# A hybrid attention and DeltaNet layer: the order of the matmuls of attention and scan written out by hand

## The chip, the cores and the metric

The kernel runs on one core of a Trainium2 chip, in one launch. The metric is the device time in microseconds, the median of the runs; the profile is one further execution, with the hardware profiler on. Engines: TensorE (PE, with its weight loads PEld), VectorE (DVE), ScalarE (ACT), GpSimd (POOL), and SyncE (SP), which here only issues DMAs.

## The reference

One layer over 1024 latent tokens (16 rows of 64) and 256 context tokens, width 1024, in float32. After an adaptive RMS norm one projection feeds two branches.

```python
# neighbourhood attention, 8 heads of 64: every latent query sees an 8 x 16 window and all context keys
s_loc = einsum('bchd,bicjhd->bhcij', q_r, k_win) + bias      # bias: learned, by row and column offset
s_ctx = einsum('bchd,bnhd->bhcn', q_r, k_ctx)
p = softmax(concatenate([s_loc, s_ctx]))                     # one softmax over both
o_na = p_loc @ v_win + p_ctx @ v_ctx
# gated DeltaNet, 4 heads of 128, forward and backward, context first, then latent
v_new = u_n - w_n @ state
o_n   = q_n @ state + qk_n @ v_new
state = state * gl_n + k_n.T @ v_new
# both branches are gated and go through one output projection
y = concatenate([o_na * silu(na_z), rmsnorm(o_g) * silu(g_z)]) @ w_out
x = x + gate * rmsnorm(y, g_post)
```

## The kernel before

The program has three stages in time. The first makes norms, projections, convolutions and the inverses of the DeltaNet chunks, and leaves queries, keys, values, gates and the scan's operands in DRAM. The second runs attention and scan side by side. The third is the output product, `phase4`.

Most products are split: a number is held as a high and a low part (`hi`, `lo`, type `F32R`), and a product is two or three matmuls. A plain float32 matmul stands in the trace as two records.

**Attention** (`na_attn`, `na_unit`). The 8 heads make 4 pairs `p`. A pair has 2 row tiles `rt` of 4 column tiles `ct`, a unit of 128 queries each. In a unit the two heads `hh` are its half units. A half unit does this:

- POOL adds the bias `gt` and the mask `mk` to `gm` (L676, 288 columns for `ct` 0 and 3, 384 for 1 and 2).
- PE makes the context scores `pc` (L684) and the local ones `pl` (L688, whose keys `kv` are read from row order `(n r c)` as `(n c r)`, that is with a stride of 64 elements).
- DVE takes the maximum (L692) and adds `gm` (L693); ACT takes both exponentials (L694, L695).
- PE transposes the result back into `pl` and `pc` (L697, L702); DVE copies it to `tl` (L699), ACT to `tcx` (L704).

After both halves the value products add up in `po` (L710, L715). After four units the row tile is scaled: DVE multiplies `po` by the gate (L610), the reciprocal sums are spread by POOL (L618) and transposed by PE (`prt`, L621, in a buffer of tag `sl`), and DVE multiplies again (L623). `pc` and `pl` have two PSUM buffers each (tags `sc`, `sl`), `po` has one.

**Scan** (`delta_scan`). Four heads, each 10 steps, both directions `d` in a step. A direction's step is a chain: `pa = kq @ state` (L1133), `y` on DVE (L1134), `pa = tm @ y` (L1138), `vn` on ACT (L1140 or L1142), `pa = kd @ vn` (L1144), new state on DVE (L1147). From the third step on it also makes outputs in `pos` (L1152, L1153), which ACT and DVE add to `o` (L1156, L1159, L1160). A head's operands are loaded at its start (`tm`, `v`, `kt`, `kq` in two buffers, `qe` in one); at its end `o` is normalised, transposed (L1182) and gated.

**What sets the order.** `phase_b` steps two Python generators: after unit `u` the scan is advanced to `min(43, u * 1.40)` steps. That is the order in which the program is written. The order in each engine's queue is then made by a planner, which follows a timeline of its own with estimated costs: of what is ready it takes what was written first. So the products of attention and scan mix freely on PE, but the mix is fixed when the program is built. An ordering edge (`order(r, before)`) ties an instruction behind another on the same queue without a semaphore.

**W_out** is cast and split into `hi` and `lo` by halves of 512 columns (`split_w`: DMA to `wor`, ACT cast L647, POOL subtraction L648), in buffers that the attention's and the scan's tiles leave (`w_out_early`), the rest in `phase4`. `phase4` multiplies in the order `W_ORDER = [3, 0, 1, 2, 4, 5, 6, 7]`: block 3 is the last pair of attention, kept on chip (`split_m`, L659, L660); blocks 0, 1, 2, 4, 5, 6 come back from DRAM through two buffers; block 7 is the last head of the scan. The last steps of the scan may run inside `phase4`, up to its sixth block.

Of the kernel before, what the change touches and what calls it, by code (L numbers as in the profile page):

```python
# [11 lines left out]
F32 = mybir.dt.float32  # L12
# [127 lines left out]
class K:  # L140
    def __init__(self, tc, I, out, dbg=None):
        self.tc, self.nc, self.I, self.out = tc, tc.nc, I, out
        self.dbg = dbg or {}
        self.na_first = None
        self.gate = self.after = None
# [438 lines left out]

    def na_attn(self, na, ps):
        nc = self.nc
# [9 lines left out]
        nxt = load(0)  # L596
        for p in range(4):
            qk, gts, vv, zs = nxt
            for rt in range(2):
                sums = self.nw.tile([P, 4, 2, 2], F32, name=f"sums{p}_{rt}", tag="sums", bufs=2)  # L600
                po = ps.tile([P, 4, P], F32, name=f"po{p}_{rt}", tag="po", bufs=1)
                for ct in range(4):
                    self.na_unit(ps, p, rt, ct, qk, vv, gts, self.mk, sums, po)
                    if p < 3 and (rt, ct) == (0, 1):
                        self.gate = self.scan_loads if p == 0 else None
                        nxt = load(p + 1)
                        self.gate = None
                    yield
                zv = zs[:, 512 * rt:512 * rt + 512].rearrange("p (a t c) -> p a t c", a=8, t=4)
                nc.vector.tensor_tensor(zv, po.rearrange("p t (a c) -> p a t c", a=8), zv, ALU.mult)  # L610
                rs = self.nw.tile([P, 8], F32, name=f"rs{p}_{rt}", tag="rs", bufs=2)
                nc.vector.tensor_tensor(rs.rearrange("p (a b) -> p a b", a=4), sums[:, :, :, 0], sums[:, :, :, 1],
                                        ALU.add)
                nc.vector.tensor_scalar(rs, rs, 2.0, None, ALU.mult)
                nc.vector.reciprocal(rs, rs)

                rb = self.nw.tile([P, 640], F32, name=f"rb{p}_{rt}", tag="pt", bufs=3)[:, :512].rearrange("p (a b) -> p a b", a=8)
                nc.gpsimd.tensor_copy(rb, bc(rs.unsqueeze(2), [P, 8, 64]))  # L618
                pt = ps.tile([P, 512], F32, name=f"prt{p}_{rt}", tag="sl", bufs=2)
                for ct in range(4):  # L620
                    nc.tensor.transpose(pt[:, ct * P:(ct + 1) * P],  # L621
                                        rb[:, 2 * ct:2 * ct + 2, :].rearrange("p a b -> p (a b)"), self.ident)
                nc.vector.tensor_tensor(zv, pt.rearrange("p (t a c) -> p a t c", t=4, a=8), zv, ALU.mult)  # L623
            if p < 3:
                self.load(self.m_dram[P * p:P * p + P, :], zs)
            else:
                self.split_m(3, zs)
            if p == 2:
                self.w_out_early(self.pf, [("qh0", 8), ("ql0", 8), ("qh1", 8), ("ql1", 8), ("kk0", 10), ("kk1", 10)])

# [10 lines left out]
    def split_w(self, k, hi, lo):  # L641
        nc = self.nc
        hr, lr = hi.bitcast(F32R), lo.bitcast(F32R)
        for o in range(0, D, 512):
            raw = self.g3.tile([P, 512], F32, name=f"wor{k}_{o}", tag="wor", bufs=2)
            self.load(raw, self.I["w_out"][k * P:(k + 1) * P, o:o + 512], self.na_last)
            nc.scalar.copy(hr[:, o:o + 512], raw)  # L647
            nc.gpsimd.tensor_tensor(lr[:, o:o + 512], raw, hi[:, o:o + 512], ALU.subtract)  # L648
        self.wo[k] = (hr, lr)
# [13 lines left out]
    def na_unit(self, ps, p, rt, ct, qk, vv, gts, mk, sums, po):  # L663
# [6 lines left out]
        tls, tcs = [], []  # L670
        for hh in range(2):
            gt = gts[hh]
            gv = bass.AP(gt.tensor, gt[:, (4 * (1 - rt)) * 31 + GCOL0[ct]:].offset,
                         [list(gt.ap[0]), [4 * 31, 3], [1, nco], [31, 4]])
            gm = self.nw.tile([P, 384], F32, name=f"gm{p}_{u}_{hh}", tag="gm", bufs=2)
            nc.gpsimd.tensor_tensor(gm[:, :n].rearrange("p (n c r) -> p n c r", c=nco, r=4), gv,  # L676
                                    mk[:, mo:mo + n].rearrange("p (n c r) -> p n c r", c=nco, r=4), ALU.add)
            pcb = ps.tile([P, 512], F32, name=f"pc{p}_{u}_{hh}", tag="sc", bufs=2)
            pl = ps.tile([P, 512], F32, name=f"pl{p}_{u}_{hh}", tag="sl", bufs=2)
            pc = pcb[:, :256]  # L680
            pl3 = pl[:, :n].rearrange("p (n c r) -> p n c r", c=nco, r=4)
            qs, kk = qk[hh]
            for i, a in enumerate(qs):
                nc.tensor.matmul(pc, a[:, u * P:(u + 1) * P], kk[:, S:S + CT], start=(i == 0), stop=(i == 1))  # L684
            kv = kk[:, 256 * rt:256 * rt + 768].rearrange("p (n r c) -> p n c r", c=64, r=4)[
                :, :, KCOL0[ct]:KCOL0[ct] + nco, :]
            for i, a in enumerate(qs):
                nc.tensor.matmul(pl3, a[:, u * P:(u + 1) * P], kv, start=(i == 0), stop=(i == 1))  # L688
            mi = self.nw.tile([P, 1], F32, name=f"mi{p}_{u}_{hh}", tag="mi", bufs=4)
            nm = self.nw.tile([P, 1], F32, name=f"nm{p}_{u}_{hh}", tag="nm", bufs=4)  # L690
            pt = self.nw.tile([P, 640], F32, name=f"pt{p}_{u}_{hh}", tag="pt", bufs=3)
            nc.vector.tensor_reduce(mi, pc, AX.X, ALU.max, negate=True)  # L692
            nc.vector.tensor_tensor_reduce(pt[:, :n], pl[:, :n], gm[:, :n], -1.0, mi, ALU.add, ALU.min, nm)  # L693
            nc.scalar.activation(pt[:, :n], pt[:, :n], AF.Exp, bias=nm, scale=-1.0, accum_out=sums[:, ct, hh, 0:1])  # L694
            nc.scalar.activation(pt[:, 384:640], pc, AF.Exp, bias=nm, accum_out=sums[:, ct, hh, 1:2])  # L695
            for rc in range(3):
                nc.tensor.transpose(pl[:m, rc * P:(rc + 1) * P], pt[:, rc * m:(rc + 1) * m], self.ident)  # L697
            tl = self.nw.tile([P, 384], F32, name=f"tl{p}_{u}_{hh}", tag="tl", bufs=4)
            nc.vector.tensor_copy(tl[:m, :], pl[:m, :384])  # L699
            tls.append(tl)  # L700
            for cc in range(2):
                nc.tensor.transpose(pc[:, cc * P:(cc + 1) * P], pt[:, 384 + cc * P:384 + (cc + 1) * P], self.ident)  # L702
            tcx = self.nw.tile([P, 2, P], F32, name=f"tcx{p}_{u}_{hh}", tag="tcx", bufs=4)
            nc.scalar.copy(tcx.rearrange("p c q -> p (c q)"), pc)  # L704
            tcs.append(tcx)

        for cc in range(2):
            for hh in (1, 0):
                hb = 64 * hh
                nc.tensor.matmul(po[hb:hb + 64, ct, :], self.vcx[:, cc, P * p + hb:P * p + hb + 64], tcs[hh][:, cc, :],  # L710
                                 start=(cc == 0), stop=False, tile_position=(0, hb))
        for rc in range(3):
            for hh in (1, 0):
                hb = 64 * hh
                nc.tensor.matmul(po[hb:hb + 64, ct, :], vv[:m, ct, rt + rc, hb:hb + 64], tls[hh][:m, rc * P:(rc + 1) * P],  # L715
                                 start=False, stop=(rc == 2), tile_position=(0, hb))
# [375 lines left out]
    def delta_scan(self, g3, ps, h):  # L1092
# [9 lines left out]
        if h == 0:  # L1102
# [4 lines left out]
            nc.gpsimd.tensor_tensor(self.rho2, self.rho, self.rho, ALU.mult)  # L1107
            yield
        tm, qe = (w.rearrange("p (d t) c -> p d t c", d=2) for w in (tm, qe))
        o = g3.tile([P, 8, P], F32, name=f"o{h}", tag="o", bufs=2)  # L1110
        if h == 3:
            self.w_out_early(g3, [("o", 8), ("tm", 20)])
        order = [list(range(10)), [1, 0] + list(range(9, 1, -1))]
        seen = set()
        st = [None, None]
        chain = [ps.tile([P, 512], F32, name=f"pa{h}_{d}", tag=f"pa{d}", bufs=1)[:, :P] for d in range(2)]
        po = ps.tile([P, 2, 2, P], F32, name=f"pos{h}", tag="os", bufs=1)
# [276 lines left out]
```

## Time and profile before

| what | value |
| --- | --- |
| median of 3 runs | 895.79 us (891.43 to 896.62) |
| profiled execution, own time | 903.52 us |
| its span in the trace | 901.8 us, mean granted clock 0.971 |
| first stage, to the first scores | 0 to 559 us |
| attention and scan, to the first output product | 559 to 801 us |
| output product and closing tiles | 801 to 902 us |

A row of the timeline is: start, duration, engine, line, operation, output<-inputs, shapes, count, and in brackets the idle time before it with what ended that. A row of the waits is: who waited, for whom, microseconds in total, times, longest. A row of a stage is: its ends, its length, busy time and instructions of PE, PEld, DVE, ACT and POOL, then the granted clock, the DMA share and GB/s.

### The profile page before, as it was taken

To read this page: it belongs to the slowest core of one execution; us is meant where nothing else is said; L and a number is where in the kernel's file an instruction comes from. 1 tells how busy PE (TensorE), PEld (TensorE's weight loads), DVE (VectorE), ACT (ScalarE), POOL (GpSimd) and SP (SyncE) were. 2 spreads that over 40 slices of the span, in tenths; PEclk is the share of its full clock that TensorE was granted. 3 is DMA by queue.
4 is the path that set the end of the run, shared out by engine and by line. 5 is a ranking of instruction groups with operands and counts; after the bars stand their busy time and mean duration, and the time that the engine had idled before them with its cause. 6 is when DMAs were issued, how large, how long until landed. Compare 5 with 4: busy or idle time off the path is not lost.

```text
span 901.8 us, 16600 instructions
## 1 busy us (share of the span) xinstructions
PE 840.9 (93%) x6082; PEld 705.1 (78%) x6082; DVE 538.4 (60%) x1179; ACT 416.5 (46%) x1165; POOL 368.9 (41%) x431
## 2 busy tenths in 40 slices
PE   5999999999999989898989977999899997899996
PEld 3688887887888868688877867888788886788785
DVE  3453464556546699679639523677677776562442
ACT  4263536645644454552243533546456555642220
POOL 1332321724544532344512112757557568532210
PEclk9999999999999989998999986999999999999999
DMA  9686432265364544633899857989759233223251
GB/s 339 252 283 243 140 117 84 82 216 177 98 228 155 136 135 153 187 105 95 283 260 260 212 172 284 356 203 256 229 138 292 98 113 121 72 87 124 92 199 61
DMA packets 95176, 160.98 MB, mean 179 GB/s; under 512 B 28581, under 2 KB 55542, under 8 KB 92918
## 3 DMA queue, kind: packets, MB, share of 16 engines
q1 hardware_dynamic: 87606, 146.25, 52.0%
q10 hardware_dynamic: 7488, 13.67, 4.9%
q8 instruction: 48, 0.79, 0.4%
q14 instruction: 34, 0.28, 0.1%
HBM read 110.82 MB, written 52.42 MB: 181 GB/s over the span
## 4 chain that ended last, share of the span: by engine, by line
PE 62%; DVE 14%; DMA 11%; ACT 5%; issue 3%; SPq 3%; POOL 1%; DVEq 0%; ACTq 0%; POOLq 0%
PE py L1218 3%; PE py L1220 3%; PE py L1219 3%; DVE tb L1003 3%; DVE vb L1006 2%; PE pl L688 2%; PE po L715 2%; PE pl L697 2%; PE pz L464 2%; PE pz L460 2%; PE pz L465 2%; PE po L710 2%; PE pc L684 2%; DMA pm_dram<-pm 2%; DMA tm_dram<-tm 2%
## 5 line engine op out<-in xcount | busy, mean ns | idle before, releaser
L676 POOL TENSOR_TENSOR gm<-gt,mk 128x288 f32<-128x288 f32 (+1 forms) x64 | 64.3, 1008 | 35.4 <-DVE nm L693 35.1
L1125 POOL TENSOR_SCALAR kd<-kt,kd 128x128 f32<-128x128 f32 x72 | 43.2, 603 | 31.2 <-PE pa L1144 30.9
L694 ACT ACTIVATE pt<-pt,nm 128x288 f32<-128x288 f32 (+1 forms) x64 | 36.7, 574 | 30.0 <-DVE nm L693 29.4
L692 DVE TENSOR_REDUCE mi<-pc 128x1 f32<-128x256 f32 x64 | 26.7, 420 | 30.8 <-PE pc L684 30.3
L945 ACT ACTIVATE em<-em,gc 128x128 f32<-128x128 f32 x80 | 25.6, 391 | 34.6 <-DMA em<-gc_dram 24.5
L699 DVE COPY tl<-pl 96x384 f32<-96x384 f32 (+1 forms) x64 | 35.3, 551 | 10.0 <-PE pl L697 9.8
L464 PE MATMUL pz<-hl,wh_gz 128*128 128x512 f32 x96 | 40.2, 418 | 0.0
L697 PE MATMUL pl<-c,pt 128*96 128x128 f32 (+1 forms) x192 | 33.0, 281 | 7.6 <-ACT pt L694 7.6
L465 PE MATMUL pz<-hh,wl_gz 128*128 128x512 f32 x96 | 39.7, 414 | 0.0
L460 PE MATMUL pz<-hh,wh_gz 128*128 128x512 f32 x96 | 39.7, 413 | 0.0
L693 DVE CUSTOM_DVE_ANT_0 pt<-pl,gm,mi 128x288 f32<-128x288 f32 (+1 forms) x64 | 35.9, 562 | 4.2 <-PE pl L688 1.5
L1003 DVE TENSOR_TENSOR tb<-ab,vb 120x31 f32<-120x31 f32 (+15 forms) x62 | 32.2, 519 | 10.3 <-DMA ab<-ab_dram 8.8
L473 PE MATMUL pv<-wh_nv,hh 128*128 128x264 f32 x128 | 35.5, 296 | 2.8 <-ACT hh L262 1.9
L475 PE MATMUL pv<-wl_nv,hh 128*128 128x264 f32 x128 | 35.8, 289 | 1.4 <-DVE wl_nv L446 1.4
L474 PE MATMUL pv<-wh_nv,hl 128*128 128x264 f32 x128 | 36.8, 292 | 0.0
L812 DVE SCALAR_TENSOR_TENSOR acc_v<-xp_v,cols,acc_v 128x1282 f32<-128x1282 f32 x16 | 29.1, 1818 | 10.8 <-ACT acc_v L810 10.6
L964 POOL TENSOR_SCALAR_AFFINE_SELECT qe<-qe 128x256 f32<-128x256 f32 x32 | 25.5, 799 | 23.4 <-DVE qe L963 22.9
L704 ACT COPY tcx<-pc 128x256 f32<-128x256 f32 x64 | 23.5, 368 | 21.6 <-PE pc L702 21.1
L960 DVE SCALAR_TENSOR_TENSOR pm<-pk,beta,em 128x128 f32<-128x128 f32 x80 | 23.6, 343 | 15.8 <-PE pk L953 11.5
L1128 POOL TENSOR_SCALAR vb<-v,beta 128x128 f32<-128x128 f32 x40 | 24.1, 604 | 17.8 <-DVE y L1134 13.9
L697 PEld LDWEIGHTS pl<-c,pt 128*96 128x96 f32 (+1 forms) x192 | 22.1, 136 | 11.9 <-ACT pt L694 10.8
L1133 PE MATMUL pa<-s,kq 128*128 128x128 f32 x144 | 28.3, 285 | 2.0 <-DVE s L1147 1.4
(438 smaller groups left out, 2903.6 us busy)
## 6 DMA issues: line engine op xcount, KB each, us to landing
wada<-in_w_ada SPq DMA_DIRECT2D x16, 512.0 KB, 6.5
em<-gc_dram SPq DMA_DIRECT2D x20, 256.0 KB, 4.1
pm_dram<-pm SPq DMA_DIRECT2D x20, 256.0 KB, 2.8
pmf<-pm_dram SPq DMA_DIRECT2D x8, 640.0 KB, 5.9
tm_dram<-tm SPq DMA_DIRECT2D x8, 640.0 KB, 7.4
kk<-qk_dram SPq DMA_DIRECT2D x16, 320.0 KB, 10.8
tm<-tm_dram SPq DMA_DIRECT2D x4, 1280.0 KB
kq_dram<-kq SPq DMA_DIRECT2D x4, 1152.0 KB
```

What stands on the lines that cost most here:

```text
L460: r = nc.tensor.matmul(ps, wh, xh, start=(k == 0), stop=False)
L464: nc.tensor.matmul(ps, wh, xl, start=False, stop=False)
L465: nc.tensor.matmul(ps, wl, xh, start=False, stop=(k == KC - 1))
L473: nc.tensor.matmul(ps, xh, wh, start=(k == 0), stop=False)
L474: nc.tensor.matmul(ps, xl, wh, start=False, stop=False)
L475: nc.tensor.matmul(ps, xh, wl, start=False, stop=(k == KC - 1))
L676: nc.gpsimd.tensor_tensor(gm[:, :n].rearrange("p (n c r) -> p n c r", c=nco, r=4), gv, mk[:, mo:mo + n].rearrange("p (n c r) -> p n c r", ...
L693: nc.vector.tensor_tensor_reduce(pt[:, :n], pl[:, :n], gm[:, :n], -1.0, mi, ALU.add, ALU.min, nm)
L694: nc.scalar.activation(pt[:, :n], pt[:, :n], AF.Exp, bias=nm, scale=-1.0, accum_out=sums[:, ct, hh, 0:1])
L697: nc.tensor.transpose(pl[:m, rc * P:(rc + 1) * P], pt[:, rc * m:(rc + 1) * m], self.ident)
L1003: nc.vector.tensor_tensor(t3, bc(ab[:, 0:m, m:m + 1], [r, m, n]), bc(vb[:, m:m + 1, m:], [r, m, n]), ALU.mult)
L1125: nc.gpsimd.tensor_scalar(kd, kt_[:, t, :], self.kd[:, h, d, t:t + 1], None, ALU.mult)
```

## The change

- `pe(r)` ties each matmul to the one before it, in the order written. It is used for all products of attention and scan, except the last head's closing transposes.
- `na_unit` is split into `na_scores`, `na_turn` and `na_values`. Round `i` of 67 writes: scores of half unit `i`; on odd rounds from 3 on the values of unit `(i-3)/2`; a slot of the scan; the transposes of half unit `i-1`; every eighth round the `prt` transposes of a row tile (now in tag `po`); on odd rounds one piece of W_out; a second slot of the scan. There are 134 slots.
- `delta_step` does both directions together and yields after each third of its chain. With the loads and the ends of heads that makes 121 slots. A head's loads are written at the fourth step of the head before; its closing transposes at the third step of the head after.
- W_out goes in pieces of 512 columns, with two loads staged ahead; each cast is tied behind the newest exponential. `phase4` loads four blocks ahead.
- `qk_out` writes the latent keys in the order `(n c r)`, so the local scores read them contiguously.
- `gm` of column tile 2 is that of column tile 1 (same mask and bias columns), with three buffers for two.

```diff
-        nc.scalar.activation(hi, src, AF.Copy, scale=scale)
-        nc.vector.scalar_tensor_tensor(lo, src, scale, hi.bitcast(F32), ALU.mult, ALU.subtract)
+        kv = lambda v, o: v.rearrange(f"p (n {o}) -> p n c r", r=4, c=64) if i and gr < 2 else v
+        nc.scalar.activation(kv(hi, "c r"), kv(src, "r c"), AF.Copy, scale=scale)
+        if i:
+            nc.vector.tensor_tensor(kv(lo, "c r"), kv(src, "r c"), kv(hi, "c r").bitcast(F32), ALU.subtract)
+        else:
+            nc.vector.scalar_tensor_tensor(lo, src, scale, hi.bitcast(F32), ALU.mult, ALU.subtract)
...
+    def pe(self, r):
+        if self.last_pe:
+            self.order(r, self.last_pe)
+        self.last_pe = r.ins.name
...
+        for i in range(2 * len(units) + 3):
+            if i < 2 * len(units):
+                j, hh = divmod(i, 2)
+                p, rt, ct = units[j]
...
+                scores[i] = self.na_scores(ps, p, rt, ct, hh, pairs[p], sums[p, rt])
+                if p < 3 and (rt, ct, hh) == (0, 2, 0):
+                    self.gate = self.scan_loads if p == 0 else None
+                    pairs[p + 1] = load(p + 1)
+                    self.gate = None
+            if i >= 3 and i % 2:
+                values((i - 3) // 2)
+            yield
+            if 1 <= i <= 2 * len(units):
+                turned[divmod(i - 1, 2)] = self.na_turn(*scores.pop(i - 1))
+            if i >= 4 and i % 8 == 2:
+                end((i - 4) // 2)
+            if i % 2:
+                self.split_piece()
+            yield
...
+        if ct != 2:
+            self.gm[hh] = self.nw.tile([P, 384], F32, name=f"gm{p}_{u}_{hh}", tag="gm", bufs=3)
...
-            kv = kk[:, 256 * rt:256 * rt + 768].rearrange("p (n r c) -> p n c r", c=64, r=4)[
-                :, :, KCOL0[ct]:KCOL0[ct] + nco, :]
+        kv = kk[:, 256 * rt:256 * rt + 768].rearrange("p (n f) -> p n f", f=256)[:, :, 4 * KCOL0[ct]:4 * KCOL0[ct] + m]
...
+    def split_piece(self, n=1):
+        nc = self.nc
+        for _ in range(min(n, len(self.staged) + len(self.pieces))):
+            raw, hi, lo = self.staged.pop(0)
+            self.order(nc.scalar.copy(hi.bitcast(F32R), raw), self.last_exp)
+            nc.gpsimd.tensor_tensor(lo.bitcast(F32R), raw, hi, ALU.subtract)
+            self.load_pieces()
...
+            for i in range(10):
+                if i == 2:
+                    for _ in ends:
+                        yield
+                    po = ps.tile([P, 2, 2, P], F32, name=f"pos{h}", tag="os", bufs=1)
+                if i == 3 and h < 3:
+                    nxt = self.delta_load(g3, h + 1)
...
+                yield from self.delta_step(g3, h, i, [w[i] for w in order], ops, st, chain, po, o, seen)
...
+    def delta_step(self, g3, h, i, ts, ops, st, chain, po, o, seen):
...
+                self.pe(nc.tensor.matmul(pa, kq[:, t, :], st[d], start=True, stop=True))
+                y.append(g3.tile([P, P], F32, name=f"y{nm[d]}", tag="yt", bufs=3))
+                nc.vector.scalar_tensor_tensor(y[d], pa, self.nsc[:, h, d, t:t + 1], vb, ALU.mult, ALU.add)
...
+        if po is not None:
+            for d, t, pa in dirs:
+                self.pe(nc.tensor.matmul(po[:, d, 0, :], kq[:, t + 8, :], st[d], start=True, stop=True))
+        if i:
             yield
...
+        for d, t, pa in dirs:
+            self.pe(nc.tensor.matmul(pa, tm[:, d, t, :], y[d], start=True, stop=True))
...
+        yield
+        if i < 9:
+            for d, t, pa in dirs:
+                self.pe(nc.tensor.matmul(pa, kd[d], vn[d], start=True, stop=True))
...
-                for u, _ in enumerate(self.na_attn(na, ps)):
-                    if u == 0:
-                        next(sc)
-                    while done < min(43, u * 1.40):
-                        next(sc)
-                        done += 1
+                for _ in self.na_attn(na, ps):
+                    next(sc, None)
```

More of the change, by code (lines that the diff above doesn't have):

```diff
@@ L594, in load @@
             return qk, gts, vv, zs
[L596 to L623, printed above, removed]
@@ new lines, in end @@
+        def end(j):
+            p, rt, _ = units[j]
+            pt = ps.tile([P, 512], F32, name=f"prt{p}_{rt}", tag="po", bufs=1)
+            for ct in range(4):
+                self.pe(nc.tensor.transpose(pt[:, ct * P:(ct + 1) * P],
+                                            rb[j][:, 2 * ct:2 * ct + 2, :].rearrange("p a b -> p (a b)"), self.ident))
+            nc.vector.tensor_tensor(row(p, rt), pt.rearrange("p (t a c) -> p a t c", t=4, a=8), row(p, rt), ALU.mult)
+            if rt == 0:
+                return
@@ new lines, in na_scores, with na_turn @@
+        self.last_exp = nc.scalar.activation(pt[:, 384:640], pc, AF.Exp, bias=nm,
+                                             accum_out=sums[:, ct, hh, 1:2]).ins.name
+        return f"{p}_{u}_{hh}", m, pc, pl, pt
+    def na_turn(self, nm, m, pc, pl, pt):
+        nc = self.nc
+        for rc in range(3):
+            self.pe(nc.tensor.transpose(pl[:m, rc * P:(rc + 1) * P], pt[:, rc * m:(rc + 1) * m], self.ident))
+        tl = self.nw.tile([P, 384], F32, name=f"tl{nm}", tag="tl", bufs=4)
+        nc.vector.tensor_copy(tl[:m, :], pl[:m, :384])
+        for cc in range(2):
+            self.pe(nc.tensor.transpose(pc[:, cc * P:(cc + 1) * P], pt[:, 384 + cc * P:384 + (cc + 1) * P], self.ident))
+        tcx = self.nw.tile([P, 2, P], F32, name=f"tcx{nm}", tag="tcx", bufs=4)
+        nc.scalar.copy(tcx.rearrange("p c q -> p (c q)"), pc)
+        return tl, tcx
@@ L1164, in delta_scan @@
-        self.dump(f"o{h}", o)
+        return kq, v, kt_, *(w.rearrange("p (d t) c -> p d t c", d=2) for w in (tm, qe))
+    def delta_scan(self, g3, ps):
+        ends = iter(())
+        order = [list(range(10)), [1, 0] + list(range(9, 1, -1))]
+        nxt = self.delta_load(g3, 0)
+        yield
+        for h in range(4):
+            ops, st, seen, po = nxt, [None, None], set(), None
+            o = g3.tile([P, 8, P], F32, name=f"o{h}", tag="o", bufs=2)
+            chain = [ps.tile([P, 512], F32, name=f"pa{h}_{d}", tag=f"pa{d}", bufs=1)[:, :P] for d in range(2)]
+            for i in range(10):
[5 more added lines that the diff above has]
+                    nxt = self.delta_load(g3, h + 1)
+                if (h, i) == (3, 1):
+                    self.w_out_early(g3, [("o", 8), ("tm", 20)])
+                yield from self.delta_step(g3, h, i, [w[i] for w in order], ops, st, chain, po, o, seen)
+            self.dump(f"o{h}", o)
+            ends = self.delta_end(g3, ps, h, o)
+            next(ends)
+        yield from ends
@@ L1230, in phase4 @@
                     new(tn, tag)
+                parts = split_in()
+                for _ in range(2):
+                    next(parts)
+                self.split_piece(2)
                 for i, k in enumerate(W_ORDER[:6]):
+                    next(parts, None)
                     if i == 3:
```

244 lines of the change are left out of this document (128 added, 116 removed).

## The prediction

> **What bounds the kernel now.** I read the page first, then busy time by stage, then the tensor queue in order of time inside the one stage that the change rewrites, then the waits there.
>
> ```profile
> PE 840.9 (93%) x6082; PEld 705.1 (78%) x6082; DVE 538.4 (60%) x1179; ACT 416.5 (46%) x1165; POOL 368.9 (41%) x431
> 0.00:555.00 555.00, 519.83 (x3662) 429.58 (x3663) 327.69 (x577) 256.49 (x611) 195.96 (x202) 0.97 0.59 185
> 559.00:801.00 242.00, 224.10 (x1964) 196.58 (x1962) 170.30 (x535) 134.41 (x490) 156.46 (x204) 0.98 0.62 184
> 801.00:902.00 101.00, 92.95 (x413) 75.03 (x412) 38.90 (x64) 24.79 (x63) 16.51 (x25) 0.98 0.36 124
> ```
>
> The columns of a stage are its ends, its length, then PE, PEld, DVE, ACT and POOL. Three stages: projections and fronts to 555, attention with the scan from 559 to 801, output products to the end. PE looks 93% busy in the middle one, but a busy PE counts a product's whole flight. How much it could issue is read from starts that follow each other without a wait:
>
> ```profile
> 650.24 0.32 PE L688 MATMUL pl<-kk,ql 128*128 128x288 f32 x1
> 650.39 0.39 PE L1133 MATMUL pa<-s,kq 128*128 128x128 f32 x2
> 650.62 0.39 PE L1152 MATMUL pos<-s,kq 128*128 128x128 f32 x2
> ...
> 652.96 0.49 PE L697 MATMUL pl<-c,pt 128*96 128x128 f32 x3
> ...
> 653.51 0.39 PE L1133 MATMUL pa<-s,kq 128*128 128x128 f32 x2
> ...
> 654.91 0.39 PE L1138 MATMUL pa<-y,tm 128*128 128x128 f32 x2
> 655.06 0.36 PE L684 MATMUL pc<-kk,qh 128*128 128x256 f32 x1
> 655.26 0.28 PE L684 MATMUL pc<-kk,ql 128*128 128x256 f32 x1
> 655.38 0.37 PE L688 MATMUL pl<-kk,qh 128*128 128x384 f32 x1
> 655.58 0.38 PE L688 MATMUL pl<-kk,ql 128*128 128x384 f32 x1
> 655.89 0.66 PE L710 MATMUL po<-tcx,vcx 128*64 128x128 f32 x8
> ...
> 657.13 0.49 PE L1152 MATMUL pos<-s,kq 128*128 128x128 f32 x2
> ```
>
> A scan product (two records) takes 0.22 (650.39 to 650.62 rounds it up), the five transposes of a half unit 0.55 (652.96 to 653.51), the value products of a unit 1.35 (655.89 to 657.13, plus 0.11 for their late start after L688). Scores: 0.12 per product on 256 keys, 0.15 on 288, 0.20 on 384, so 0.54 or 0.65 a half unit, mean 0.60. By the loops there are 64 half units, 32 units, 352 scan products (72, 80 and 72 on the chain, 64 and 64 for outputs) and 64 single transposes of 0.11. Sum: 64 x 0.60 + 64 x 0.55 + 32 x 1.35 + 352 x 0.22 + 64 x 0.11 = 38.4 + 35.2 + 43.2 + 77.4 + 7.0 = 201, of which some 3 us (the last step, the last head's eight transposes) come after 801. So 198 us of issue fill 242: **44 us are lost to waits**, and these are what a better order can win. The last stage has no such room: PE is busy 92.95 of its 101 us, and the rest is mostly the closing tile.
>
> ```profile
> PE pl L697 <- ACT pt L694: 7.6, 10, 1.5
> PE po L710 <- ACT tcx L704: 3.1, 2, 2.9
> ...
> 770.51 0.37 PE L688 MATMUL pl<-kk,ql 128*128 128x384 f32 x1
> 772.61 0.62 ACT L647 CAST wo_o<-wor 128x512 fp32r<-128x512 f32 x1 [2.93 <-DMA wor<-in_w_out]
> 773.40 0.36 ACT L704 COPY tcx<-pc 128x256 f32<-128x256 f32 x1
> 773.81 0.66 PE L710 MATMUL po<-tcx,vcx 128*64 128x128 f32 x8 [2.93 <-ACT tcx L704]
> 775.30:778.70 3.40, 3.31 (x15) 3.02 (x15) 2.15 (x6) 1.79 (x8) 3.30 (x4) 0.50 0.50 154
> ```
>
> The visible waits are PE on ACT: transposes on the exponentials, values on the copied transposes. The worst case reads off in order: the cast of a W_out piece stands in ACT's queue ahead of its DMA, ACT idles 2.93, the copy comes late, PE idles 2.93, and right after that the granted clock is 0.50 for 3.4 us.
>
> **The change part by part.** (1) *The order.* Each half unit becomes: its scores, on odd ones the values of an older unit, a third of a scan step, the transposes of the half unit before, another third. Nothing is computed more or less; what counts is how much each result may age before PE asks for it. The lengths of the links:
>
> ```profile
> 689.64 0.60 DVE L693 CUSTOM_DVE_ANT_0 pt<-pl,gm,mi 128x384 f32<-128x384 f32 x1
> 689.73 0.37 ACT L704 COPY tcx<-pc 128x256 f32<-128x256 f32 x1
> ...
> 690.29 0.62 ACT L694 ACTIVATE pt<-pt,nm 128x384 f32<-128x384 f32 x1 [0.19 <-DVE nm L693]
> 690.90 0.45 ACT L695 ACTIVATE pt<-pc,nm 128x256 f32<-128x256 f32 x1
> 691.26 0.19 ACT L695 ACTIVATION_READ_ACCUMULATOR pt<-pc,nm 128x1 f32 x1
> ...
> 692.08 0.39 PE L684 MATMUL pc<-kk,qh 128*128 128x256 f32 x1
> 692.62 0.42 DVE L692 TENSOR_REDUCE mi<-pc 128x1 f32<-128x256 f32 x1 [1.29 <-PE pc L684]
> ...
> 693.96 0.35 DVE L1134 SCALAR_TENSOR_TENSOR y<-pa,nsc,v 128x128 f32<-128x128 f32 x1
> ```
>
> From scores to maxima 0.54, the maxima 0.42, from the sum with the bias to the end of both exponentials 1.81 (689.64 to 691.45): 2.8 us until a half unit can be transposed. PE has about 4.5 us of its own work (one set of scores, one of values, one of transposes, three thirds) before it asks. Good. A link of the scan is 0.4 in PE (0.11 + 0.28), 0.35 in DVE for one direction and 0.3 more for the other, some 1.0; between thirds PE has at least the transposes, 0.55, and the rest of the third, 0.2 to 0.7. Just enough. The tight link is another: scores take the PSUM buffer that the copy tcx of two half units back must have left. On an even half unit (no values) PE's own work is 0.60 + 0.55 + two thirds (1.3 to 1.8) = 2.4 to 2.9, but ACT first finishes that half unit's exponentials, 0.54 + 0.42 + 1.81, and then the copy, 0.37, with a few hundredths between: 3.2. So an even half unit loses 0.3 to 0.7, mean 0.6. Odd ones own about 4 and lose 0.15 (one scan link in three stands behind an exponential). That is 0.75 a pair, for 29 pairs **22 us**. I take it between two bounds: 8 us if the copy slips in between the two exponentials (0.45 and 0.19 sooner), and 39 if the stage waits as it does now (44 less the 2.9 us hole and some 2 at its start).
>
> (2) *The ends.* The scan has 121 slots of the 134, so the last six rounds run without it, and the last pair's chain stands open, where before scan products lay in it:
>
> ```profile
> 797.76 0.71 PE L1133 MATMUL pa<-s,kq 128*128 128x128 f32 x4
> 797.88 0.69 DVE L610 TENSOR_TENSOR zs<-po,zs 128x512 f32<-128x512 f32 x1 [0.67 <-PE po L715]
> ...
> 798.76 0.60 PE L621 MATMUL prt<-c,rb 128*128 128x128 f32 x4
> ...
> 799.40 0.69 DVE L623 TENSOR_TENSOR zs<-prt,zs 128x512 f32<-128x512 f32 x1
> ...
> 800.17 1.04 ACT L659 CAST m<-zs 128x1024 fp32r<-128x1024 f32 x1
> ...
> 801.26 1.66 PE L1218 MATMUL py<-wo_qh,m 128*128 128x512 f32 x6
> ```
>
> 0.69 + 0.60 + 0.69 + 1.04 less 0.44 of transposes is 3 us with PE empty (the transposes now also wait for the buffer that L610 reads); the last exponentials and copies uncovered cost 2 more: **5 us**, between 2 and 8. Such a pause ended in a half clock above: 3.4 us at half speed, **1.7 us** more, between 0 and 3.4. [...]
>
> At the start the first scan product is fixed in the second slot, ahead of the second half unit:
>
> ```profile
> 559.58 0.58 PE L684 MATMUL pc<-kk,qh 128*128 128x256 f32 x1
> 563.35 0.55 PE L1138 MATMUL pa<-v,tm 128*128 128x128 f32 x2
> ```
>
> Today a second set of scores and a transposition lie in these 3.8 us; then only one: **4 us** lost in all (2 to 6).
>
> (3) *W_out in pieces*, one on every second half unit with two loads staged ahead: the 2.9 us hole goes; it is inside the 44. (4) *Loads of the next head* at its fourth step, five issues on SP. On SP they now stand behind the pair loads, zs and zg that come before that step. The single buffer of qe is free only at the head's end; its first use is eight slots, 8 x 228 / 134 or some 13 us, later, and those slots hide it. I cost it at nothing; if SP is held before it, it costs the transfer, 1 MB at the stage's 184 GB/s, some 6 us a head.
>
> (5) *Keys regrouped.* L688 gets contiguous keys. 0.12 per 256 gives 0.135 and 0.18 instead of 0.15 and 0.20: 64 x 0.015 + 64 x 0.02, **2.2 us** won (0 to 4). The eight casts and eight subtractions of 512 columns that now read PSUM with a stride lie in the first stage, where ACT is idle for 298 and DVE for 227 of 555 us. The nearest strided read of that size, L610, takes 0.69; even were all sixteen twice as long, 11 us would lie beside PE: nothing, and a few tenths where one is late.
>
> (6) *Shared bias sum*, 16 of 64 sums of about 1 us on POOL:
>
> ```profile
> POOL gm L676 <- DVE nm L693: 35.1, 21, 12.1
> ```
>
> POOL waits 35 us there for its readers, so the sums are not late now: nothing.
>
> Sum: 44 - 22 - 5 - 1.7 - 4 + 2.2 = 13.5 us won. The profiled run's 903.5 becomes 890; the median of the runs, 895.8, becomes **882**. (About 1%, 9 us, is what a measurement of this kernel tells from no change.)
>
> **The rivals.** *The copies slip in* (0.15): the stage loses 8 instead of 22 and the gain is 28: 868. For it: ACT is busy 134 of 242, and exponentials of one half unit do not always stand together. *DVE becomes the bound* (0.24): its 170 us stay, so a stage of 228 has it 75% busy instead of 70%, in one queue with the scan's links; one 0.4 us wait behind a copy or a sum per pair adds 12, and it is 893: no change. For it: the slack of a link is a few tenths. Against: DVE has 58 us free. *ACT's queue sets the pace* (0.18): if a scan copy or two (0.37 each) also stand ahead of the tcx copy on even half units, the pair loses 1.5 to 1.8, the stage 48, and the kernel is slower by 12: 908. It decides from 1.2 us a pair (13.5 more over 29 pairs than my 0.75). Against: such copies come ready before the exponentials more often than behind them. That the order does not take effect has no share: every product of attention and scan is tied to the one before.
>
> **How the numbers follow.** Forecast 0.43 at 882, its own range 874 to 888. Range over all: 866 takes in the copies that slip in; 904 takes in most of DVE's case and the smaller half of ACT's. Faster by over 1%: 0.43 + 0.15 less a little = 0.57; within: 0.24; slower: 0.19.
>
> **What would show it.** The stage from first scores to first output product shrinks from 242 to about 228, ahead of an unchanged last stage. In the waits: scores on the copy (pc on tcx) become the largest of PE, on every second half unit; transposes on the exponentials vanish. L688's starts are 0.135 and 0.18 apart. No hole at W_out casts; a hole of 3 to 5 us before the first output product, then clock 0.50. Wrong makes me: PE waits spread over DVE's y and s, SP holding a head's loads, or a first stage that moved by more than 3 us.

## The result, and the profile after

The changed kernel is slower: 952.98 us median (949.15 to 954.40) against 895.78, a ratio of 1.0642 with a 95% interval of 1.0595 to 1.0690. The forecast was 882, in a range of 866 to 904. The profiled run of after took 949.15 us, its span is 947.0.

The page of after, then busy time by stage in the columns of the prediction; the stages are projections, attention with scan, output products.

```profile
PE 840.2 (89%) x6082; PEld 706.1 (75%) x6082; DVE 543.2 (57%) x1179; ACT 416.9 (44%) x1165; POOL 352.1 (37%) x415
0.00:546.50 546.50, 517.19 (x3714) 429.01 (x3714) 327.54 (x580) 257.97 (x613) 193.54 (x200) 0.98 0.60 191
546.50:849.00 302.50, 232.02 (x1985) 203.79 (x1984) 181.15 (x551) 137.60 (x508) 143.85 (x193) 0.93 0.51 154
849.00:947.00 98.00, 90.98 (x388) 73.26 (x386) 34.50 (x49) 21.37 (x45) 14.67 (x22) 0.97 0.30 105
```

Every engine's busy time is within 5 us of before, but for POOL's, 17 us less. The stage of attention and scan grew from 242 to 302.5 us, and its clock fell from 0.98 to 0.93. The forecast expected 228; some 74 us are missing. The first stage looks 12 us shorter, but that is not the change: the unchanged kernel, profiled once more, has it at 549.5.

```profile
0.00:549.50 549.50, 524.02 (x3715) 433.56 (x3715) 327.65 (x580) 257.89 (x613) 194.73 (x202) 0.96 0.60 190
549.50:789.70 240.20, 222.84 (x1959) 195.29 (x1958) 170.16 (x536) 134.93 (x491) 156.41 (x204) 0.99 0.61 185
789.70:890.30 100.60, 92.78 (x412) 74.83 (x411) 38.83 (x64) 24.66 (x63) 16.36 (x25) 0.98 0.38 124
```

Against this trace the stages of after differ by -3.0, +62.3 and -2.6, together 56.7; the medians differ by 57.2. So the whole loss lies in the stage that the change orders. What PE waits for there, in after:

```profile
PE pos L1215 <- DVE o L1245: 36.8, 22, 10.3
PE ot L1268 <- POOL o L1260: 13.8, 3, 6.0
PE pc L733 <- ACT tcx L757: 6.8, 14, 0.9
PE pl L751 <- ACT pt L743: 3.0, 1, 3.0
PE ot L1268 <- DVE o L1265: 2.2, 1, 2.2
```

The first two rows are new. Neither the prediction's sum nor its rivals name them. L1215 writes the scan's output products on the old state into `pos`; L1268 is the closing transpose of a head. Before, the planner had put other products ahead of one that had to wait; that trace has 0.5 us of waits at `pos` and none at `ot`. Here the timeline of after shows one of the 22 waits at `pos`:

```profile
592.89 0.61 PE L1208 MATMUL pa<-s,kq 128*128 128x128 f32 x4
...
593.71 0.68 DVE L639 TENSOR_TENSOR zs<-prt,zs 128x512 f32<-128x512 f32 x1
594.30 0.34 DVE L1210 SCALAR_TENSOR_TENSOR y<-pa,nsc,v 128x128 f32<-128x128 f32 x1
594.56 0.34 DVE L1210 SCALAR_TENSOR_TENSOR y<-pa,nsc,vb 128x128 f32<-128x128 f32 x1
594.82 0.28 DVE L1245 TENSOR_TENSOR o<-pos,o 128x128 f32<-128x128 f32 x1
...
595.15 0.60 PE L1215 MATMUL pos<-s,kq 128*128 128x128 f32 x3 [1.65 <-DVE o L1245]
```

`pos` has one PSUM buffer. The order has the products that write it first (L1215) in the first third of a step, one slot behind the last third of the step before, which filled it. Its readers on ACT and DVE (two directions, two operations each) have not finished: the last is in DVE's queue behind a row tile's scaling and both `y`. PE stands, for the order lets nothing pass. The row understates it: 1.82 us pass from the last issue (592.89 and four records of 0.11) to 595.15, and it says 1.65, since a product's flight counts as busy (0.61 us in that row, for 0.44 of issue).

The longest of the 22 is a W_out cast:

```profile
774.18 0.71 PE L1208 MATMUL pa<-s,kq 128*128 128x128 f32 x4
...
776.60 0.32 SPq L154 DMA_DIRECT2D zs<-z_dram  x1
776.97 13.10 SPq L154 DMA_DIRECT2D wor<-in_w_out  x5
...
783.17 0.62 ACT L697 CAST wo_o<-wor 128x512 fp32r<-128x512 f32 x1 [8.06 <-DMA wor<-in_w_out]
783.69 0.36 ACT L1241 ACTIVATE o<-pos,egc 128x128 f32<-128x128 f32 x1
...
784.09 0.29 DVE L1245 TENSOR_TENSOR o<-pos,o 128x128 f32<-128x128 f32 x1 [8.77 <-ACT o L1241]
...
785.21 1.22 PE L1215 MATMUL pos<-s,kq 128*128 128x128 f32 x4 [10.32 <-DVE o L1245]
```

The cast of a piece is tied to its place behind an exponential, but its load stands on SP behind `zs` of the last pair, whose single buffer has just been stored. ACT waits 8.06 us for the load, the scan's output waits behind the cast, PE waits for the output. It is the hole of 2.93 us of before, three times as long. And a head's end, once in each of three heads:

```profile
761.00 1.90 POOL L1260 TENSOR_TENSOR o<-o,rq_y_o 128x1024 f32<-128x1024 f32 x1
...
762.95 1.12 PE L1268 MATMUL ot<-c,o 128*128 128x128 f32 x4 [5.99 <-POOL o L1260]
762.90:766.40 3.50, 3.45 (x22) 3.17 (x24) 1.61 (x4) 0.48 (x2) 0.98 (x2) 0.50 0.00 0
785.20:788.70 3.50, 3.16 (x14) 2.87 (x14) 0.56 (x1) 0.96 (x3) 1.43 (x2) 0.50 0.49 147
595.10:598.60 3.50, 3.45 (x36) 3.04 (x37) 1.05 (x3) 1.20 (x5) 0.50 (x1) 1.00 0.00 0
```

The last three rows are stretches of 3.5 us behind three pauses: behind 5.99 and 10.32 us the clock is 0.50, behind 1.65 it is 1.00. So these two pauses are paid twice: the four records right behind them take 1.12 and 1.22 us, those at 592.89 took 0.61.

### The profile page after: what moved, and what is told of

Its sections match the earlier page's. It is cut to its first block, busy times and chain, and to the rows that moved or that the text cites. A ratio compares the mean times of both kernels' runs of the same rounds, so it can differ in the third digit from the quotient of the medians.

```text
span 947.0 us, 16574 instructions
## 1 busy us (share of the span) xinstructions
PE 840.2 (89%) x6082; PEld 706.1 (75%) x6082; DVE 543.2 (57%) x1179; ACT 416.9 (44%) x1165; POOL 352.1 (37%) x415
## 4 chain that ended last, share of the span: by engine, by line
PE 56%; DVE 17%; DMA 10%; ACT 6%; POOL 4%; issue 3%; SPq 2%; DVEq 0%; POOLq 0%; ACTq 0%
PE py L1318 3%; PE py L1320 3%; PE py L1319 3%; DVE tb L1060 3%; DVE vb L1063 3%; PE pc L733 2%; PE pos L1215 2%; PE pz L465 2%; PE pz L461 2%; PE pz L466 2%; PE pl L736 2%; DVE pt L742 1%; ACT pt L743 1%; PE po L771 1%; DMA pm_dram<-pm 1%
## 5 line engine op out<-in xcount | busy, mean ns | idle before, releaser
L726 POOL TENSOR_TENSOR gm<-gt,mk 128x288 f32<-128x288 f32 (+1 forms) x48 | 46.2, 968 | 52.2 <-DVE nm L742 52.1
L1215 PE MATMUL pos<-s,kq 128*128 128x128 f32 x128 | 22.4, 299 | 36.8 <-DVE o L1245 36.8
L1215 PEld LDWEIGHTS pos<-s,kq 128*128 128x128 f32 x128 | 17.1, 194 | 41.1 <-DVE o L1245 41.0
L1373 DVE TENSOR_TENSOR finv<-py,ggb 128x512 f32<-128x512 f32 x16 | 11.0, 690 | 54.1 <-ACT finv L1372 53.7
L1372 ACT ACTIVATE finv<-py 128x512 f32<-128x512 f32 x16 | 9.6, 599 | 61.4 <-PE py L1320 45.3
L1060 DVE TENSOR_TENSOR tb<-ab,vb 120x31 f32<-120x31 f32 (+15 forms) x62 | 30.3, 488 | 8.5 <-DMA ab<-ab_dram 6.9
L1021 POOL TENSOR_SCALAR_AFFINE_SELECT qe<-qe 128x256 f32<-128x256 f32 x32 | 25.5, 801 | 22.9 <-DVE qe L1020 22.8
```

Source lines behind the costliest of these rows:

```text
L726: nc.gpsimd.tensor_tensor(self.gm[hh][:, :n].rearrange("p (n c r) -> p n c r", c=nco, r=4), gv, self.mk[:, mo:mo + n].rearrange("p (n c r) ...
L1060: nc.vector.tensor_tensor(t3, bc(ab[:, 0:m, m:m + 1], [r, m, n]), bc(vb[:, m:m + 1, m:], [r, m, n]), ALU.mult)
L1215: self.pe(nc.tensor.matmul(po[:, d, 0, :], kq[:, t + 8, :], st[d], start=True, stop=True))
```

## The experiments

The theory: a written order does not itself cost anything, but each product must stand late enough behind all that it needs. Three things stood too early: the products into `pos`, the closing transposes and the W_out casts. The rivals: the scores' tight link of the prediction, or the two other edits (keys, bias sum) carry the loss. The versions e1 to e6 add up, each holds the one before. Medians are beside a kernel before of 894 us in each set of runs.

**e1: products on the old state in the last third.** The step keeps the state that it began with.

```diff
-        if po is not None:
-            for d, t, pa in dirs:
-                self.pe(nc.tensor.matmul(po[:, d, 0, :], kq[:, t + 8, :], st[d], start=True, stop=True))
+        was = list(st)
...
         if po is not None:
+            for d, t, pa in dirs:
+                self.pe(nc.tensor.matmul(po[:, d, 0, :], kq[:, t + 8, :], was[d], start=True, stop=True))
```

> The two output products on the old state move from the first third of a step to its last, beside the other two. Theory (the single buffer pos sets the pace: its readers on ACT and DVE finish some 1.5 us after PE asks for it again, 28 steps): the wait of pos on o, 36.8 us in the changed kernel, falls under 5, and the stage of attention and scan goes from 302 to 265-275; the 10 us hole at the W_out cast stays, since it then only meets another product. Rival (DVE's queue is late as a whole, the buffer only happens to be where it shows): the wait moves to y and s, and the stage stays at 295-302.

Measured: 921.27 us, ratio 1.033 (1.029 to 1.036); the stage takes 270.1. Waits of e1:

```profile
PE ot L1268 <- POOL o L1260: 14.7, 3, 6.0
PE pos L1235 <- DVE o L1245: 4.8, 1, 4.8
```

Of 36.8 us in 22 waits one of 4.8 is left, at the W_out cast (10.3 in after, expected to stay as it was). This one shift is worth 32 us of the stage and 30 to 32 of the medians (30 with each beside its own kernel before), more than half of the loss.

**e2: closing transposes two slots later**, behind the second third of the third step.

```diff
-                if i == 2:
-                    for _ in ends:
-                        yield
...
+                if i == 2:
+                    for _ in range(2):
+                        next(step)
+                        yield
+                    for _ in ends:
+                        yield
```

> On top of the run before: the closing transposes of a head stand two slots later, behind the second third of the next head's third step. Theory (their normalisation takes some 12 us over ACT, DVE and POOL and is simply asked for too early, 4 to 6 us at each of three heads, with a half clock behind it): the waits of ot on o fall from 13.8 us to under 5, and the kernel gains 8-14 us over the run before. Rival (POOL is too busy and takes the transposes' place in its queue whenever they come): the wait stays over 10 and nothing is gained.

Measured: 909.94 us, ratio 1.021 (1.015 to 1.027), stage 261.0: 11.3 us gained. In its waits the closing transposes fall by half, not under 5:

```profile
PE ot L1273 <- POOL o L1265: 7.4, 3, 3.4
```

**e3: W_out pieces late**, only from round 53 on, and three at the start of `phase4` instead of two.

```diff
-            if i % 2:
+            if i % 2 and i >= 53:
                 self.split_piece()
```

> On top of the run before: pieces of W_out are cast from round 53 on, not 47. Theory (a cast stands in ACT's queue before its load can start, since the load is behind the last pair's gate load on SP, which waits for a store that PE has yet to feed; 10.3 us of PE idle and a half clock): the hole at 775 to 785 goes, 9-13 us gained. Rival (the loads are slow, whenever the cast comes): the hole moves to the later rounds and nothing is gained.

Measured: 906.14 us, ratio 1.015 (1.009 to 1.021), stage 250.8 at a clock of 0.97. The stage of its trace is 10.2 shorter, but the median fell by 3.8 only, for 9 to 13 expected. The runs spread from 900.3 to 910.4 and the traced one is the fastest of the four, so what this shift is worth stays between the two. The waits of e3 have no `pos` left, 7.4 us at the closing transposes as in e2, and:

```profile
PE pc L733 <- ACT tcx L757: 5.1, 11, 1.0
```

Three shifts have taken the stage from 302.5 to 250.8. The link that the prediction did count remains, here one pair in the timeline of e3:

```profile
641.18 0.62 PE L1221 MATMUL pa<-y,tm 128*128 128x128 f32 x4
641.43 0.37 ACT L757 COPY tcx<-pc 128x256 f32<-128x256 f32 x1 [0.36 <-PE pc L755]
...
641.86 0.39 PE L733 MATMUL pc<-kk,qh 128*128 128x256 f32 x1
...
644.35 0.61 PE L1212 MATMUL pa<-s,kq 128*128 128x128 f32 x4
645.00 0.37 ACT L757 COPY tcx<-pc 128x256 f32<-128x256 f32 x1
...
645.42 0.38 PE L733 MATMUL pc<-kk,qh 128*128 128x256 f32 x1 [0.46 <-ACT tcx L757]
```

Four records of 0.11 before each set of scores end their issue at 641.62 and 644.79. So the scores lose 0.24 and 0.63, this pair 0.87, where the prediction said 0.15 and 0.60. The waits show 0.46 of it: the 0.24 are hidden in the flight of the product before, which ends at 641.80.

**k2: keys and bias sum as before, in the order of e3.**

```diff
-        kv = kk[:, 256 * rt:256 * rt + 768].rearrange("p (n f) -> p n f", f=256)[:, :, 4 * KCOL0[ct]:4 * KCOL0[ct] + m]
+        kv = kk[:, 256 * rt:256 * rt + 768].rearrange("p (n r c) -> p n c r", c=64, r=4)[
+            :, :, KCOL0[ct]:KCOL0[ct] + nco, :]
...
-        if ct != 2:
+        if True:
```

> The third of the cumulative versions (products on the old state in the last third, closing transposes two slots later, W_out pieces late) with the keys and the bias sum put back as before, under the same written order. Theory: in a fixed order these two edits are worth little, the regrouped keys 2.2 us in the stage of attention and scan (scores 0.12 and 0.18 apart against 0.135 and 0.20) and the shared sum nothing, so this runs 0 to 3 us slower than that version: stage 251 to 254, 904 to 909. The 15 us that the two edits cost by themselves without the order came from the planner's other mix. Rival: the two edits themselves cost 10 us or more, by the strided casts or the longer life of the sums: then this is 10 to 15 us faster than that version, 890 to 896.

Measured: 907.90 us, ratio 1.011 (1.007 to 1.016), stage 255.2. Against e3 the medians do not differ by what the runs can tell; the stage is 4.4 longer, 255.2 where 251 to 254 was expected. Half of that is the starts of the local scores, in k2 and then in after:

```profile
639.97 0.37 PE L734 MATMUL pl<-kk,qh 128*128 128x384 f32 x1
640.17 0.37 PE L734 MATMUL pl<-kk,ql 128*128 128x384 f32 x1
```
```profile
590.66 0.34 PE L736 MATMUL pl<-kk,qh 128*128 128x384 f32 x1
590.84 0.34 PE L736 MATMUL pl<-kk,ql 128*128 128x384 f32 x1
```

0.20 against 0.18, as predicted. The two edits are not the loss.

**b1: the kernel before with the two edits alone**, no written order.

> The kernel before with the regrouped keys and the shared bias sum alone, no order written out. Theory (both are small, the loss is all in the order): local scores start 0.135 and 0.18 apart, 2 us gained of PE's work, time within 890-896. Rival (the strided casts cost the first stage something, or POOL's relief frees more than its own time): 897-905, or under 886.

A miss: 909.62 us, ratio 1.019 (1.015 to 1.024), stage 259.1, so 15 us slower. Waits of PE and the queue of ACT in b1:

```profile
PE pc L690 <- ACT tcx L709: 6.2, 2, 5.7
PE pos L1157 <- DVE o L1165: 5.3, 5, 3.3
752.39 0.62 ACT L652 CAST wo_qh<-wor 128x512 fp32r<-128x512 f32 x1 [5.22 <-DMA wor<-in_w_out]
```

Shorter instructions change the planner's timeline, and with it what it puts where: the cast of a W_out piece now stands ahead of a copy, with its load late, and PE idles 5.7 us. Since k2 shows the same edits worth nothing or a little in the other direction in a fixed order, the 15 us belong to the planner's other mix; the two holes, 5.7 and 3.3, account for 9 us of its stage, which is 18.9 longer than in b0. Behind the longer one the twelve value products of a unit took 1.55 us (758.08), those of a later unit 0.82 (766.25), and the page of b1 has the clock at 7 and 8 tenths in its two slices from 748.5 to 793.9 us, by which I estimate 7 us more.

**e4: context transposes ahead of local ones**, so that the copy to `tcx` starts sooner.

```diff
+        for cc in range(2):
+            self.pe(nc.tensor.transpose(pc[:, cc * P:(cc + 1) * P], pt[:, 384 + cc * P:384 + (cc + 1) * P], self.ident))
...
+        nc.scalar.copy(tcx.rearrange("p c q -> p (c q)"), pc)
         for rc in range(3):
             self.pe(nc.tensor.transpose(pl[:m, rc * P:(rc + 1) * P], pt[:, rc * m:(rc + 1) * m], self.ident))
...
```

> The third cumulative version, and the transposes of the context part ahead of those of the local part. The copy to tcx then starts some 0.33 us earlier, and the scores that wait for it lose 0.6 us per even half unit less 0.33, and 0.15 per odd one less all of it. Theory: of the 21 us lost at the scores 10 to 13 go; stage 251 to 239 or 241, 893 to 898. Rival: the copy stands behind the next exps on ScalarE and comes no earlier: under 4 us gained, 902 to 907.

A miss: 904.58 us, ratio 1.009 (1.006 to 1.012), 1.6 us under e3. The time is in the rival's range, but not for its reason, since the copy does come sooner. The stage is 255.0 for e3's 250.8; part of that is that this trace is of the slowest of four runs (905.60) and e3's of the fastest. Its waits say what happened:

```profile
PE ot L1273 <- POOL o L1265: 10.0, 3, 4.0
PE pc L733 <- ACT tcx L753: 1.5, 6, 0.4
PE pl L736 <- DVE tl L757: 1.0, 4, 0.3
```

The wait on ACT's copy went, from 5.1 to 1.5, and 1.0 of it came back one matmul later: the local scores wait for the other copy, `tl`, whose transposes now come last. At the heads' ends, which depend on POOL and not on the copy, the wait grew from 7.4 to 10.0, and the stage's clock fell from 0.97 to 0.94.

**e5: value products behind the transposes and split**, the context part in odd rounds, the local part in even ones (in a row tile's last unit both in the odd one).

```diff
-            if i >= 3 and i % 2:
-                values((i - 3) // 2)
             yield
             if 1 <= i <= 2 * len(units):
                 turned[divmod(i - 1, 2)] = self.na_turn(*scores.pop(i - 1))
+            j = (i - 3) // 2
+            if i >= 3 and i % 2:
+                values(j, 0)
+            if j >= 0 and (units[j][2] == 3) == (i % 2 == 1):
+                values(j, 1)
```

> The version before (context first), and the value products moved behind the transposes and split: the context part in odd rounds, the local part in the even rounds after. Every half unit then has some 0.45 us of values between the transposes and the scores that wait for their copy. Theory: the waits of the scores fall under 4 us in sum, stage 233 to 238, 886 to 893. Rival: the values, now sooner behind their own copies, or the scan's thirds take the wait over: under 3 us gained over the version before, or slower.

Measured: 898.15 us, ratio 1.003 (1.001 to 1.005), stage 245.5, 9.5 under e4. The median gained 6.4 over e4, which is about what the two expectations had between them, but from a worse start, so the 886 to 893 is missed; the waits for the copy are down to one, and the heads' ends are the largest:

```profile
PE ot L1276 <- POOL o L1268: 10.0, 3, 3.7
PE pc L736 <- ACT tcx L756: 0.9, 1, 0.9
```

**e6: the heads' ends and the start.** Squares are taken as a block of outputs is complete, the normalisation is in halves, and two bias sums go ahead of the scan's first `kd` on POOL.

```diff
+                if i > 5:
+                    sq, var = self.osq[h]
+                    nc.scalar.activation(sq, ot, AF.Square, accum_out=var[:, t - 2:t - 1])
...
-            nc.gpsimd.tensor_tensor(o, o, bc(r.unsqueeze(2), [P, 8, P]), ALU.mult)
+            for sl in (slice(0, 4), slice(4, 8)):
+                nc.gpsimd.tensor_tensor(o[:, sl], o[:, sl], bc(r[:, sl].unsqueeze(2), [P, 4, P]), ALU.mult)
...
+                if h == 0 and i < 2:
+                    self.order(k, self.first_gm)
```

> The version before (context first, values split), and three edits at its largest waits that are left: the squares of a head's outputs are taken as each block of outputs is complete and not eight in a row at the head's end; its normalisation on GpSimd is in two halves, so that the first closing transposes wait for the first only; and the bias sums of the first two half units stand ahead of the scan's first kd on GpSimd's queue. Theory: the heads' closing transposes lose 1 us or less instead of 3.1 to 3.7 at each of three heads, with the slow clock after them, 7 to 10 us in sum, and the start 3 us: stage 245 to 233 or 236, 885 to 890, under the kernel before. Rival: the squares, now between the scan's steps, hold ScalarE's copies to vn and tcx up, or closing waits on GpSimd's queue as before: under 4 us gained, 894 to 899.

Measured: **882.39 us** (879.18 to 887.50), ratio 0.986 (0.983 to 0.990): faster than both kernels. Its stage and two of its waits:

```profile
549.30:782.00 232.70, 222.22 (x1986) 194.91 (x1985) 179.08 (x553) 138.38 (x508) 142.20 (x195) 0.98 0.64 194
PE pa L1232 <- DVE y L1225: 1.9, 5, 0.7
PE ot L1285 <- POOL o L1277: 0.9, 1, 0.9
```

That is a little better than expected. 10.0 us at the heads' ends became 0.9, the transposes' wait on the exponentials, 4.4 in e5 with 3.5 at the start, became 0.4, the clock is back at 0.98, and the stage is 7.5 shorter than that of the kernel before, 70 shorter than after's, with the same products. No wait shows that the squares between the steps hold the scan up.

**e7: e6 with the value products ahead of the next scores**, and the `prt` transposes one round later, since the values that they follow end later.

```diff
+            j = (i - 4) // 2
+            if i >= 4 and i % 2 == 0:
+                values(j, 0)
...
-            if i >= 4 and i % 8 == 2:
-                end((i - 4) // 2)
+            if i >= 4 and i % 8 == 3:
+                end((i - 5) // 2)
```

> The version before (squares, bias ahead), and the value products stand ahead of the scores of the next half unit instead of behind the transposes, past one third of a scan step. The scores have the same 0.45 us more between the transposes and themselves; the scan's thirds have 0.55 and 1.1 us of attention between them alternately instead of 0.65 and 1.0, and the value products one third more behind their copies. Theory: the waits of the second and last thirds stay within 2 us of the version before: same to 2 us either way. Rival: the copies' waits or the thirds' move by more than 4 us.

A miss: 893.20 us, ratio 0.999 (0.997 to 1.002), stage 241.2.

```profile
PE pa L1232 <- DVE y L1225: 5.1, 15, 1.9
PE po L771 <- DVE zs L639: 3.4, 4, 1.4
```

The next row tile's values wait for the buffer of `prt`, which DVE reads just before them, and the scan's second third waits longer on `y`: 6.6 us of the stage's 8.5. It is the fault of after once more, a writer set one slot behind its buffer's readers. The other 4.0 us of the span, in the first stage, are not explained.

**b0: the kernel before, again.**

> The kernel before, unchanged, profiled once more. In its first trace the stage of the projections ran to 559.6 us and that of attention and scan for 241.7; every later trace of the other kernels has the first stage at 547 to 551. Theory: that first trace was a long one and nothing of the first stage belongs to the change: first stage 546 to 551 here, attention and scan 240 to 244, span 886 to 896. Rival: the rewriting moves the first stage by 8 to 12 us as well: first stage 557 to 562 again.

Measured: 894.56 us, stages 549.5, 240.2 and 100.6, shown above: the theory's numbers.

## Why the prediction was wrong

- **Reading of before: right.** 44 us of waits in a stage of 198 us of issue. e6 shows that an order can win some of them: 7.5 us of stage.
- **(1) The order: here it failed.** The step followed the chain of the scan and the buffers of `pc` and `pl`, found one tight link and gave it all the loss. That link was well sized (0.87 against 0.75 in the pair shown). But the same question, who has to have left the buffer, was not asked of `pos`, though one buffer and the new place of L1215 stood in the diff: 36.8 us of waits, 32 of them worth a stage of 32 (e1). Nor was it asked when a closing transpose can start, which the text never prices: 13.8 us in three heads and 2.2 in the last.
- **What these places leave open.** With the three shifts of e1 to e3 the stage is 51.7 us shorter, but still 22.8 above the 228 of the forecast, and e3 is slower than before. Its waits have 7.4 us at the heads' ends and 5.6 on the scan's own links (`pa` on `vn` 2.6, on `y` 1.7, on `kd` 1.3), which the sum called just enough and put at nothing. The rest of the 22.8 is not divided up.
- **(2) The ends: right in size at the tail, in part by luck, and blind in the middle.** In the last 6 us of the stage PE idles 4.1 and the clock is low, in after:

```profile
843.00:849.00 6.00, 1.90 (x10) 1.26 (x9) 4.71 (x5) 1.08 (x2) 3.65 (x4) 0.67 0.59 218
843.84 3.44 DVE L1265 TENSOR_TENSOR o<-o,rq_y_o 128x512 f32<-128x512 f32 x2 [1.23 <-POOL rq_y_o L1258]
...
847.21 0.68 DVE L639 TENSOR_TENSOR zs<-prt,zs 128x512 f32<-128x512 f32 x1
```

  The chain of the last pair does stand open there, but its scaling L639 stands in DVE's queue behind the last head's normalisation (L1265, 3.44 us), which the sum does not have. And each other head has an end too; these three lie within the stage. The start cost 3.0 by the wait on the exponentials, in the range of 2 to 6.
- **The half clock was mis-sized.** It was charged once, 1.7 us. In after the heads' ends (pauses of 3.98, 3.80 and 5.99 us) have a clock of 0.56, 0.56 and 0.50 in the 3.5 us behind them, the W_out hole 0.50 and then 0.75 in the 3.5 and 3.3 us behind it; from these rows I estimate 7 us. The stage's mean of 0.93 against 0.99 in b0 holds the pauses' own time too. It fits that e2 gains more (9.1 of stage, its clock 0.95 for e1's 0.92) than the waits that it removes (7.3). The sum had one such pause, at the tail; after has these four besides, of 3.80 to 10.32 us.
- **(3) W_out in pieces: wrong in sign.** "The 2.9 us hole goes"; it became 10.3. Fixing the cast's place does not fix that of its load on SP.
- **(4) and (6): nothing, as said**, as far as the trace shows: PE's waits name neither `qe` nor `gm`. SP's order does matter, but through W_out; and the sums matter at the start, by their place in POOL's queue (e6).
- **(5) Keys: right**, 0.18 for 0.20; 2.2 us by the starts, too little for the medians to tell.
- **The rivals.** "ACT's queue sets the pace, slower" had the right sign for another reason: ACT is 137.60 us busy of 302.5. None of the three was what happened: two varied the one link that the sum held, the third was DVE's queue as a whole, and none asked who has to leave `pos`.
- **What would show it.** That the scores' wait on the copy would be PE's largest failed: in after it is third (6.8), in e3, with `pos` gone, second (5.1); e4 and e5 were made to remove it. The transposes' wait on the exponentials went from 7.6 to 3.0, one, at the start.

That e6 ends at 882 is not the forecast come true: it has edits that the change lacks, and its stage still lies 35 us above the 198 of issue.

## What to carry to other kernels

When an order of products is fixed by hand, list for every product both what it reads and who must have left the buffer that it writes, with the queue that these readers stand in, and place the writers of a single buffer as late in the step as their result allows; the same holds for a cast whose load is on another queue (8.06 us of ACT in after). Before, the planner's mix hid such waits by putting other products ahead (0.5 us of waits at `pos`); in an order by hand the first product that stands too early stops all behind it (36.8 us). To price a small edit, hold the order still, as in k2: the same edit in a planned kernel (b1) moves the mix and measures that.

## What the runs showed of the hardware

In after the pauses of TensorE of 5.99 us and of 10.32 us were followed by 3.5 us and more at a clock of 0.50, one of 1.65 us by none. Among shorter ones length alone did not decide: one of 1.73 us in after (to 316.59) had 1.00 in the 3.5 us behind it, one of 1.41 us in before (to 21.34, with pauses of 0.89 and 0.19 us in the 4 us ahead of it) had 0.57. The pause of 2.93 us in before had 3.4 us at 0.50 behind it, 1.5 us after the products had started again.

After had 22 waits at one product; no buffer was added, its place in the step was enough (36.8 to 4.8 us). One program gave a first stage of 559 us in one trace and 549.5 in another: a stage that the change does not touch can differ by 10 us between two profiled executions (the record does not say whether on one chip), and should be profiled twice before it is explained.
